# A two-layer gated DeltaNet and Conformer encoder on one core: the small-tile products of two delta steps stand side by side, and the filling comes in three groups a step

## Chip, core and metric

One core of one Trainium2 chip. The metric is the device time of one execution in microseconds (us). A core has a matrix engine (TensorE, PE in the rows; PEld is its weight load), a vector engine (VectorE, DVE), an engine for functions of one operand (ScalarE, ACT), a general one (GpSimd, POOL) and one that issues transfers (SyncE, SP). Each takes its instructions in order from its own queue; semaphores tie them together. Operands lie in SBUF, products arrive in PSUM.

## What is computed

Two layers over 2048 tokens of width 1024. Each has an input projection, a bidirectional gated DeltaNet (4 heads of 128), a Conformer convolution branch, gates, two output projections and a residual sum. The change lies in the DeltaNet's scan over chunks, which the reference writes so:

```python
lmat = jnp.where(strict, jnp.einsum('bhncd,bhnsd->bhncs', k_beta, k) * decay, 0.0)
sol = lax.linalg.triangular_solve(eye + lmat, rhs, left_side=True, lower=True, unit_diagonal=True)
value, k_cum = sol[..., :dv], sol[..., dv:]
attn = jnp.einsum('bhncd,bhnsd->bhncs', q, k) * decay
...
def step(state, inp):
    val_n, kc_n, a_n, qd_n, kd_n, dl_n = inp
    v_new = val_n - jnp.einsum('bhcd,bhde->bhce', kc_n, state)
    o_n = jnp.einsum('bhcd,bhde->bhce', qd_n, state) + jnp.einsum('bhcs,bhse->bhce', a_n, v_new)
    state = state * dl_n[..., None, None] + jnp.einsum('bhcd,bhce->bhde', kd_n, v_new)
    return state, o_n
```

It runs once forward and once backward, and the two outputs are added, normalised and gated.

## The kernel before

The layer first makes all projections (`head`, `conformer`, `act_tile`, `gates(0)`), then runs `delta`, then `merge`. Wide products are split into three f32r matmuls of 128x512 (lines 185 to 187: high times high, high times low, low times high) for each 128 rows of the contraction.

`delta` takes 128 tokens per chunk and works in 16 steps; step s treats chunk s forward and chunk 15-s backward. Three kinds of generators are advanced by hand in the loop, and that written order is bound on TensorE, ScalarE, VectorE and GpSimd (`bind`); the transfers of SP are placed by the scheduler.

- `lane(step, d, ...)`, one per direction, is the scan itself: pk and pq (keys and queries times the state, L989 and L992), the x update on VectorE (L994) and o1 on ScalarE (L998); from step 8 on a sum on GpSimd (L1001) with the output that the other direction left for this chunk; pw (the inverse times x, L1005) and its copy to vn (L1007); pn and po (L1014, L1023), the state update (L1017) and the output sum (L1025 or L1030).
- `prep(i)` makes the inverse of the 128x128 triangular matrices of step i from the inverses of its 32x32 blocks, ahead of time. Its pieces are: loads; masks on GpSimd (L907); exponentials on ScalarE (L913); then transposes (L917), copies (L923, and pp on L925) and products with the decays (L927, L929); then four small-tile phases on TensorE: z1 (32x32, L936), do (32x32, L946 and L949), z2 (64x64, L960 and L961), d2 (64x64, L969 and L970), each followed by copies out of PSUM (L939; L951 to L955; L963; L971 and L972). Each `go(i)` advances prep(i) by one piece.
- `finish(pair)` from step 8 on normalises two finished outputs: squares on ScalarE (L1044); one step later the rsqrt chain on VectorE (L1054, L1055, L201 to L207, L1058), the scaling on ScalarE (L1062), and transposes on TensorE (L1067) with the gate's product on VectorE (L1068).

Between them `pull(n)` takes n filling units out of other work: the second half of the gates, then the first part of the merge. A unit is three 128x512 matmuls. Eight of them make one output tile (evicted by L829 on ScalarE, with a store issued there, L153), and every sixteen a new weight is split into halves, by ScalarE (L159) and VectorE (L160).

All products but the filling use one pool of five PSUM tiles (pz) in turn; the filling has three of its own (pd). The operands of prep lie in rings: two steps of keys (rgk), three of queries (rgq), two of row decays (rgb), three of inverses (rwt).

Of the kernel before, what the change touches and what calls it, by code (L numbers as in the profile page):

```python
# [27 lines left out]
GAP = 0  # L28
SPLITS = (245, 247, 249, 250, 251, 252, 253, 254)
LEAD = (8, 10, 6, 6, 6, 4)  # L30
STEP = (4, 4, 4, 4)
TAIL = (2, 2, 1, 4, 8)
Z = '121'
PART = 5
# [44 lines left out]
class Trunk:  # L79
# [754 lines left out]
    def delta(self):  # L834
        nc = self.nc
# [6 lines left out]
        def ring(cols, n):  # L842
            out = []
            for _ in range(n):
                slot = next(x for x in left if x[2] - x[1] >= cols)
                out.append(slot[0][:, slot[1]:slot[1] + cols])
                slot[1] += cols
            return Ring(out)

        rkq, rkv = ring(1024, 4), ring(1024, 4)  # L850
        rgq, rgk = ring(NB, 6), ring(NB, 4)
        rwt = ring(1024, 3)
        rgb, ro1, rvn, ro, rza, rst, dp = (ring(NB, n) for n in (4, 2, 2, 5, 2, 2, 2))
# [5 lines left out]
        hv = lambda t: t.rearrange("p (h c) -> p h c", h=4)  # L859

        def fetch(step):
            out = []
            for d in range(2):
                c = step if d == 0 else NCH - 1 - step
                kq = rkq().rearrange("p (h a c) -> p h a c", h=4, a=2)
                kv = rkv().rearrange("p (a h c) -> p a h c", h=4, a=2)
                self.load(kq, self.kq_d[c])
                self.load(kv, self.kv_d[c])
                out.append((c, kq, kv))
            return out  # L870

        def decay_keys(ins, d):
            c, _, kv = ins
            k2 = col(self.kf, d, c)
            nc.gpsimd.tensor_tensor(out=kv[:, 0], in0=kv[:, 0], in1=k2[:, :, None].to_broadcast([P, 4, P]),
                                    op=ALU.mult)
# [7 lines left out]
        def prep(step):  # L884
            ins, ks, gbs = [], [], []
# [2 lines left out]
            pt = dpt[:, 256:512].rearrange("p (d h c) -> p d h c", d=2, h=4)  # L888
            chunk = (step, NCH - 1 - step)
            for d, c in enumerate(chunk):  # L890
                g, k, gb = hv(rgq()), hv(rgk()), hv(rgb())
                with nc.allow_non_contiguous_dma(reason="rows to all partitions and inverse blocks"):
                    r0 = d * 64 + c * 4
                    self.load(gb, self.gc_d[r0:r0 + 4][None].to_broadcast([P, 4, P]))
                    self.load(k, self.g_d[c][:, :, 0, :])
                    self.load(g, self.g_d[c][:, :, 1, :])
                    r4 = 64 * d + 4 * c
                    self.load((dt if d == 0 else pt)[:, d],
                              self.inv_d[:, r4:r4 + 4, :].rearrange("h b (i j) -> (b i) h j", j=32))
                ins.append(g)  # L900
                ks.append(k)
                gbs.append(gb)
            yield
            for d, c in enumerate(chunk):
                gb = gbs[d]
# [3 lines left out]
            for d, c in enumerate(chunk):  # L909
                gb = gbs[d]  # L910
# [10 lines left out]
            for b in range(4):  # L921
                r = blk(b)
                v_.tensor_copy(wt[r, :, 32 * b:32 * b + 32], dtm[r])  # L923
                d, q = (0, 32 * b) if b < 2 else (1, 32 * (b - 2))
# [150 lines left out]
        def pull(n):  # L1075
            for _ in range(n):
                if next(fill, GAP) == GAP:
                    return

        start = self.mark()  # L1080
        nil = iter(())
        preps = [prep(i) for i in range(NCH)] + [nil, nil, nil]
        go = lambda i: next(preps[i], None)
        go(0)
        ins = fetch(0)
        pull(LEAD[0])
        go(0)
        go(0)
        go(0)
        go(1)  # L1090
        pull(LEAD[1])
        go(0)
# [3 lines left out]
        pull(LEAD[2])  # L1096
        go(1)
        go(0)
        pull(LEAD[3])
        go(1)  # L1100
        go(0)
        go(2)
        pull(LEAD[4])
        ready = go(0)
        pull(LEAD[5])
        last = finish([])
        for step in range(NCH):
            nxt = fetch(step + 1) if step + 1 < NCH else None
            gs, wt = ready
            lanes = [lane(step, d, gs[d], wt, *ins[d]) for d in range(2)]  # L1110
            for x in lanes:
                next(x)
            go(step + 1)
            go(step + 2)
            for x in lanes:
                next(x)
            if nxt:
                for d in range(2):
                    decay_keys(nxt[d], d)
            next(last)  # L1120
            pull(STEP[0])
            for x in lanes:
                next(x)
            go(step + 2)
            next(last)
            go(step + 1)
            pull(STEP[1])
            for x in lanes:
                next(x, None)
            go(step + 1)  # L1130
            go(step + 2)
            go(step + 3)
            new = finish(list(done))
            done.clear()
            if step == NCH - 1:
                break
            if step < LATE_SQUARES:
                next(new)
            pull(STEP[2])
            if step >= LATE_SQUARES:  # L1140
                next(new)
            next(last)
            ready = go(step + 1)
            last = new
            pull(STEP[3])
            ins = nxt
        for n, part in zip(TAIL, (new, last, new, new, new)):
            pull(n)
# [351 lines left out]
```

## Time and profile before

| | |
|---|---|
| median of three runs | 3140.98 us (3136.1 to 3143.68) |
| profiled execution, its time | 3143.1 us |
| its span, first to last instruction | 3141.3 us |
| TensorE clock granted over the span | 0.995 |
| delta stage, layer 1: first pw of step 0 | at 910.8 us |
| delta stage, layer 2: first pw of step 0, of step 15 | at 2447.5 and 2787.5 us |

A row of the timeline reads: start, duration, engine, line, operation, output <- input, shape, count; in brackets the engine's idle time before it and what ended that. A PE duration is longer than the distance to the next start, since matmuls are pipelined: distances of starts are what counts there. A row of a single line gives minimum/median/maximum duration in ns. In the chain each row is start, duration and line of a piece of the work that ended last.

### The profile page before, as it was taken

The numbers are of one execution on the slowest core, as the hardware profiler recorded it, in microseconds if no ns is written. First come the engines' busy times: TensorE is split into PE (matmuls) and PEld (weight loads), VectorE is DVE, ScalarE is ACT, GpSimd is POOL, SyncE is SP. The second block draws the span as 40 slices with busy tenths as digits, with TensorE's granted clock in tenths as the row PEclk, the third lists the DMA queues.
The fourth block names the chain that finished last, engine by engine and source line by source line (L and its number), as shares of the span: only waits on it lengthen the run. The fifth ranks groups of instructions, "written<-read, shape, count | busy, mean of one in ns | idle before, by whom it ended". The sixth has DMA issues, their size and how long they took to land. (4 is left out here: it accounts for less than half of the span.)

```text
span 3141.3 us, 51438 instructions
## 1 busy us (share of the span) xinstructions
PE 3077.3 (98%) x19190; PEld 2707.1 (86%) x19190; DVE 2400.3 (76%) x4441; ACT 1377.3 (44%) x3074; POOL 297.9 (9%) x297
## 2 busy tenths in 40 slices
PE   6999999999999999999999999999999999999998
PEld 5888888888889998888888888888888899988887
DVE  7789898997556698746666989999955567877665
ACT  5625152522454466434345252525234545644342
POOL 3000000000032222000000000000001212200000
PEclk9999999999999999999999999999999999999999
DMA  4233222234587787655413141414347878965643
GB/s 147 90 95 95 88 91 91 89 111 137 194 297 253 250 266 237 198 188 141 152 35 106 67 124 58 121 61 119 124 158 258 269 234 266 290 201 189 216 159 124
DMA packets 429417, 501.71 MB, mean 160 GB/s; under 512 B 96432, under 2 KB 262960, under 8 KB 429168
## 3 DMA queue, kind: packets, MB, share of 16 engines
q1 hardware_dynamic: 351232, 380.19, 38.8%
q10 hardware_dynamic: 69872, 88.48, 8.0%
q0 software_dynamic: 8064, 29.76, 2.5%
q8 instruction: 151, 2.47, 0.3%
q14 instruction: 98, 0.80, 0.1%
HBM read 342.74 MB, written 155.58 MB: 159 GB/s over the span
## 5 line engine op out<-in xcount | busy, mean ns | idle before, releaser
L185 PE MATMUL pd<-h,whi 128*128 128x512 f32 x2816 | 1092.3, 388 | 0.0
L187 PE MATMUL pd<-h,wlo 128*128 128x512 f32 x2816 | 1070.5, 380 | 1.5 <-DVE wlo L160 1.5
L186 PE MATMUL pd<-h,whi 128*128 128x512 f32 x2816 | 1070.9, 380 | 0.0
L749 DVE SCALAR_TENSOR_TENSOR cacc<-gp,vec,cacc 128x1009 f32<-128x1009 f32 (+1 forms) x480 | 615.7, 1283 | 29.6 <-ACT cacc L747 26.6
L185 PEld LDWEIGHTS pd<-h,whi 128*128 128x128 f32 x2816 | 534.1, 190 | 79.5 <-issue 1.4
L187 PEld LDWEIGHTS pd<-h,wlo 128*128 128x128 f32 x2816 | 533.7, 190 | 78.6 <-DVE wlo L160 2.3
L186 PEld LDWEIGHTS pd<-h,whi 128*128 128x128 f32 x2816 | 534.0, 190 | 72.6 <-issue 1.9
L159 ACT ACTIVATE whi<-wraw 128x512 fp32r<-128x512 f32 x394 | 239.3, 623 | 478.6 <-PE pd L186 352.6
L160 DVE TENSOR_TENSOR wlo<-wraw,whi 128x512 fp32r<-128x512 f32 x394 | 267.8, 693 | 116.9 <-ACT whi L159 115.2
L574 DVE SCALAR_TENSOR_TENSOR acc<-cin,vec,acc 128x1022 f32<-128x1022 f32 (+1 forms) x192 | 246.5, 1299 | 13.9 <-ACT acc L572 12.6
L187 PE MATMUL pd<-yhi,wlo 128*128 128x512 f32 x488 | 185.6, 380 | 4.6 <-DVE wlo L160 4.5
L185 PE MATMUL pd<-yhi,whi 128*128 128x512 f32 x488 | 185.5, 380 | 0.7 <-ACT whi L159 0.7
L186 PE MATMUL pd<-ylo,whi 128*128 128x512 f32 x488 | 185.0, 379 | 0.0
L829 ACT ACTIVATE go<-pd,vec 128x512 f32<-128x512 f32 x128 | 87.3, 682 | 130.9 <-PE pd L187 116.6
L550 ACT ACTIVATE cin<-pd 128x512 f32<-128x512 f32 x96 | 56.8, 593 | 152.3 <-PE pd L187 152.1
L761 ACT ACTIVATE ao<-pd 128x512 f32<-128x512 f32 x64 | 38.3, 599 | 193.9 <-PE pd L187 193.8
L187 PEld LDWEIGHTS pd<-yhi,wlo 128*128 128x128 f32 x488 | 92.2, 189 | 19.5 <-DVE wlo L160 6.6
L185 PE MATMUL pd<-uop,whi 128*128 128x512 f32 x256 | 100.2, 391 | 5.1 <-ACT whi L159 5.1
L185 PEld LDWEIGHTS pd<-yhi,whi 128*128 128x128 f32 x488 | 92.2, 189 | 14.3 <-ACT whi L159 1.5
L186 PEld LDWEIGHTS pd<-ylo,whi 128*128 128x128 f32 x488 | 92.2, 189 | 12.9
L187 PE MATMUL pd<-uop,wlo 128*128 128x512 f32 x256 | 98.0, 383 | 0.1
L186 PE MATMUL pd<-uop,whi 128*128 128x512 f32 x256 | 97.8, 382 | 0.0
(312 smaller groups left out, 4814.9 us busy)
## 6 DMA issues: line engine op xcount, KB each, us to landing
wraw<-w_in SPq DMA_DIRECT2D x240, 256.0 KB, 3.5
gt<-go ACTq DMA_DIRECT2D x128, 256.0 KB, 4.2
dl<-gr SPq DMA_DIRECT2D x128, 256.0 KB, 5.3
dl<-kq SPq DMA_DIRECT2D x64, 512.0 KB, 6.3
dl<-kv SPq DMA_DIRECT2D x64, 512.0 KB, 5.7
wraw<-w_out SPq DMA_DIRECT2D x90, 256.0 KB, 3.0
kq<-acc SPq DMA_DIRECT2D x16, 1024.0 KB, 5.4
gr<-go ACTq DMA_DIRECT2D x64, 256.0 KB, 2.2
```

What stands on the lines that cost most here:

```text
L159: self.nc.scalar.activation(hi, src, AF.Copy)
L160: self.nc.vector.tensor_tensor(out=lo, in0=src, in1=hi.bitcast(F32), op=ALU.subtract)
L185: mm(ps, whi[:, k, :], xhi, start=k == 0, stop=False)
L186: mm(ps, whi[:, k, :], xlo, start=False, stop=False)
L187: mm(ps, wlo[:, k, :], xhi, start=False, stop=k == kk - 1)
L550: nc.scalar.activation(cut(t[:, o + b * NB:o + (b + 1) * NB]), sort(ps), AF.Copy)
L574: self.nc.vector.scalar_tensor_tensor(out=out, in0=t[:, k:k + n], scalar=wc(k), in1=out, op0=ALU.mult, op1=ALU.add)
L749: self.nc.vector.scalar_tensor_tensor(out=acc, in0=t[:, k:k + n], scalar=wc(k), in1=acc, op0=ALU.mult, op1=ALU.add)
L761: nc.scalar.activation(cut(o), sort(ps), func)
L829: nc.scalar.activation(cut(o), sort(ps), AF.Identity if half else AF.Sigmoid, bias=self.vec[:, V_GB + j:V_GB + j + 1])
```

## The change

Prep's loads become two pieces (the row decays first, then k, queries and inverse blocks), so that prep has nine pieces for eight. The loop advances them in another order, and a step's sixteen filling units come as 6, 5 and 5 in place of 4, 4, 4 and 4. The start of the stage is rewritten to match.

```diff
-STEP = (4, 4, 4, 4)
+STEP = (6, 5, 5)
...
             for d, c in enumerate(chunk):
-                g, k, gb = hv(rgq()), hv(rgk()), hv(rgb())
+                gb = hv(rgb())
...
                     self.load(gb, self.gc_d[r0:r0 + 4][None].to_broadcast([P, 4, P]))
+                gbs.append(gb)
+            yield
+            for d, c in enumerate(chunk):
+                g, k = hv(rgq()), hv(rgk())
...
                     self.load(k, self.g_d[c][:, :, 0, :])
                     self.load(g, self.g_d[c][:, :, 1, :])
...
             for x in lanes:
                 next(x)
-            go(step + 1)
             go(step + 2)
             for x in lanes:
                 next(x)
             if nxt:
                 for d in range(2):
                     decay_keys(nxt[d], d)
+            go(step + 2)
             next(last)
             pull(STEP[0])
             for x in lanes:
                 next(x)
-            go(step + 2)
+            go(step + 3)
             next(last)
-            go(step + 1)
             pull(STEP[1])
             for x in lanes:
                 next(x, None)
             go(step + 1)
             go(step + 2)
             go(step + 3)
...
             next(last)
+            go(step + 2)
             ready = go(step + 1)
+            go(step + 3)
             last = new
-            pull(STEP[3])
```

In step s the loop now makes of prep(s+2) the exponentials, then the transposes, copies and products, then z1 and do; of prep(s+1) z2 and d2; of prep(s+3) both loads and the masks.

TensorE in one step of layer 1, before, from the output products (L1023) to pw (L1005) of the next step; rows of L185 to L187 are filling:

```order
L1023 MATMUL pz<-dm_6983,dl_6981 128x128 x4
L960 MATMUL pz<-dh_6988,dl_6981 64x64
L961 MATMUL pz<-dh_6988,dl_6981 64x64
...
L185 MATMUL pd<-h_395,whi 128x512
...
L969 MATMUL pz<-dl_6981,dh_6989 64x64
L970 MATMUL pz<-dl_6981,dh_6989 64x64
...
L185 MATMUL pd<-h_395,whi 128x512
...
L992 MATMUL pz<-dh_6987,dl_6980 128x128 x4
L936 MATMUL pz<-dh_6987,dl_6981 32x32 x16
```

The same stretch now (every line behind the loads carries a number four higher: z2 is L964 and L965, z1 L940, do L950 and L953, d2 L973 and L974, pk L993):

```order
L1027 MATMUL pz<-dm_6983,dl_6981 128x128 x4
L964 MATMUL pz<-dh_6988,dl_6981 64x64
L965 MATMUL pz<-dh_6988,dl_6981 64x64
...
L940 MATMUL pz<-dh_6987,dl_6981 32x32 x16
L185 MATMUL pd<-h_395,whi 128x512
...
L953 MATMUL pz<-dh_6989,dh_6987 32x32 x2
L973 MATMUL pz<-dl_6981,dh_6989 64x64
L974 MATMUL pz<-dl_6981,dh_6989 64x64
...
L993 MATMUL pz<-dh_6986,dl_6980 128x128 x4
```

z1 has moved from behind pq to behind z2, do from behind pw to just ahead of d2, and no filling is left between d2 and the next step's pk.

VectorE in a late step of layer 1 (step 9), before, from the x update to the copies of d2:

```order
L994 SCALAR_TENSOR_TENSOR dl_6980<-pz,neg,dl_6980 128x128 x8
L1054 TENSOR_TENSOR oss<-oss,cq_1007 128x8
...
L1058 TENSOR_TENSOR orr<-orr,cq 128x8
L951 COPY dh_6988<-pz 32x4x32
...
L1017 SCALAR_TENSOR_TENSOR dh_6986<-dh_6986,dl,pz 128x128 x4
...
L917 STREAM_TRANSPOSE dh_6988<-dh_6988 128x128 x2
L923 COPY dl_6981<-dh_6988 32x8x32 x4
L927 TENSOR_TENSOR dl_6981<-dl_6981,dm_6982 128x512 x2
L929 TENSOR_TENSOR dl_6981<-dl_6981,dm_6982 128x512 x2
L160 TENSOR_TENSOR wlo<-wraw,whi 128x512 x2
L1068 SCALAR_TENSOR_TENSOR dh_6985<-pz,vec,dh_6985 128x512
```

And now:

```order
L998 SCALAR_TENSOR_TENSOR dl_6980<-pz,neg,dl_6980 128x128 x8
L921 STREAM_TRANSPOSE dh_6988<-dh_6988 128x128 x2
L927 COPY dl_6981<-dh_6988 32x8x32 x4
L931 TENSOR_TENSOR dl_6981<-dl_6981,dm_6982 128x512 x2
L933 TENSOR_TENSOR dl_6981<-dl_6981,dm_6982 128x512 x2
L1058 TENSOR_TENSOR oss<-oss,cq_1007 128x8
...
L1062 TENSOR_TENSOR orr<-orr,cq 128x8
L160 TENSOR_TENSOR wlo<-wraw,whi 128x512 x2
L1021 SCALAR_TENSOR_TENSOR dh_6986<-dh_6986,dl,pz 128x128 x4
...
L1072 SCALAR_TENSOR_TENSOR dh_6985<-pz,vec,dh_6985 128x512
...
L955 COPY dh_6988<-pz 32x4x32
```

The transposes, copies and products stand ahead of the rsqrt chain, and the weight split (L160) ahead of the state update.

ScalarE in the same step, before, from vn (L1007) to the next eviction:

```order
L1007 ACTIVATE dm_6983<-pz 128x512 x2
L913 ACTIVATE dm_6982<-dm_6982,ngc 128x128 x8
L1062 ACTIVATE dm_6984<-dm_6984,orr 128x128 x8
L829 ACTIVATE go<-pd,vec 128x512
...
L963 ACTIVATE dh_6989<-pz 128x256
L925 ACTIVATE dh_6988<-dh_6988 32x4x32 x4
...
L159 ACTIVATE whi<-wraw 128x512 x2
```

And now, from the exponentials:

```order
L917 ACTIVATE dm_6982<-dm_6982,ngc 128x128 x8
L929 ACTIVATE dh_6988<-dh_6988 32x4x32 x4
L1011 ACTIVATE dm_6983<-pz 128x512 x2
L1066 ACTIVATE dm_6984<-dm_6984,orr 128x128 x8
L829 ACTIVATE go<-pd,vec 128x512
...
L159 ACTIVATE whi<-wraw 128x512 x2
L967 ACTIVATE dh_6989<-pz 128x256
L943 ACTIVATE dh_6989<-pz 128x128
L1048 ACTIVATE junk,oss<-dh_6985 128x128 x4
```

The exponentials and pp come ahead of vn, and the weight's first half (L159) ahead of the squares (L1044, now L1048), right behind the scaling and an eviction.

More of the change, by code (lines that the diff above doesn't have):

```diff
@@ L890, in prep @@
             for d, c in enumerate(chunk):
-                g, k, gb = hv(rgq()), hv(rgk()), hv(rgb())
-                with nc.allow_non_contiguous_dma(reason="rows to all partitions and inverse blocks"):
+                gb = hv(rgb())
+                with nc.allow_non_contiguous_dma(reason="rows to all partitions"):
                     r0 = d * 64 + c * 4
                     self.load(gb, self.gc_d[r0:r0 + 4][None].to_broadcast([P, 4, P]))
+                gbs.append(gb)
+            yield
+            for d, c in enumerate(chunk):
+                g, k = hv(rgq()), hv(rgk())
+                with nc.allow_non_contiguous_dma(reason="inverse blocks"):
                     self.load(k, self.g_d[c][:, :, 0, :])
@@ L901, in prep @@
                 ks.append(k)
-                gbs.append(gb)
             yield
@@ L1084, in delta @@
         go(0)
+        go(0)
         ins = fetch(0)
@@ L1089, in delta @@
         go(0)
+        go(1)
         go(1)
@@ L1098, in delta @@
         go(0)
+        go(1)
         pull(LEAD[3])
+        go(0)
         go(1)
-        go(0)
+        go(2)
         go(2)
@@ L1104, in delta @@
         ready = go(0)
+        go(1)
+        go(2)
         pull(LEAD[5])
```

## The prediction

> **What bounds the kernel now.** I read the page's engine shares first, then TensorE's timeline through one step of the delta stage, then VectorE's, ScalarE's and GpSimd's timelines through a late step, then the waits and the chain.
>
> ```profile
> PE 3077.3 (98%) x19190; PEld 2707.1 (86%) x19190; DVE 2400.3 (76%) x4441; ACT 1377.3 (44%) x3074; POOL 297.9 (9%) x297
> ```
>
> TensorE is busy nearly throughout, so only two things can move the time: how tightly its instructions follow each other, and the few places where it waits. The change touches TensorE's order in the two delta stages alone (16 steps each).
>
> ```profile
> 2455.32 1.06 PE L1023 MATMUL pz<-dm,dl 128*128 128x128 f32 x8
> 2456.31 0.27 PE L960 MATMUL pz<-dh,dl 64*64 64x64 f32 x1
> ...
> 2456.77 0.22 PE L961 MATMUL pz<-dh,dl 64*64 64x64 f32 x1
> 2456.92 0.48 PE L185 MATMUL pd<-h,whi 128*128 128x512 f32 x1
> 2457.24 0.38 PE L186 MATMUL pd<-h,whi 128*128 128x512 f32 x1
> 2457.46 0.38 PE L187 MATMUL pd<-h,wlo 128*128 128x512 f32 x1
> ```
>
> This is one small-tile phase, z2, between full-width work. Eight L1023 at 0.11 us each end at 2456.21; the first 64x64 matmul starts 0.10 us later. After the last one 0.15 us pass, and the first filling matmul holds TensorE 0.32 us where its successor takes 0.22: 0.10 more. The phase thus costs 0.81 us (2456.21 to 2457.02), of which its sixteen matmuls stream for about 0.47. **About 0.34 us is getting in and out.**
>
> The late steps look different:
>
> ```profile
> 2647.77 1.78 PE pz L1005 x16
> ...
> 2717.66 1.78 PE pz L1005 x16
> 2740.77 1.80 PE pz L1005 x16
> ...
> 2765.17 1.78 PE pz L1005 x16
> ```
>
> These pieces of the chain are the pw products of steps 9, 12, 13 and 14. From 12 to 13 a step takes 23.11 us with TensorE never waiting; from 9 to 12 the three take 69.89, 0.5 more than three such; from 13 to 14 24.40, 1.3 more. **So 1.8 us per layer are lost to waits in late steps already.** One of them has its name in the waits:
>
> ```profile
> PE pz L989 <- DVE dh L1068: 0.8, 1, 0.8
> ```
>
> The pool of five pz tiles is used in turn: a state product (L989) had to wait until VectorE had read the transposed output (L1068) out of the tile five before it. VectorE, ScalarE and GpSimd around that place:
>
> ```profile
> 2644.14 1.27 POOL L1001 TENSOR_TENSOR dm<-dm,dm 128x512 f32<-128x512 f32 x1 [14.75 <-ACT dm L998]
> 2645.92 1.27 POOL L1001 TENSOR_TENSOR dh<-dh,dm 128x512 f32<-128x512 f32 x1 [0.51 <-ACT dm L998]
> 2647.15 2.04 POOL L875 TENSOR_TENSOR dl<-dl,kf 128x512 f32<-128x512 f32 x2
> 2649.15 2.51 POOL L907 TENSOR_TENSOR dm<-dm,con 128x512 f32<-128x512 f32 x2
> ```
> ```profile
> 2645.95 1.27 DVE L205 TENSOR_TENSOR rst<-orr,rsv 128x8 f32<-128x8 f32 x1
> ...
> 2652.51 0.17 DVE L1058 TENSOR_TENSOR orr<-orr,cq 128x8 f32<-128x8 f32 x1
> ...
> 2654.55 1.12 DVE L1017 SCALAR_TENSOR_TENSOR dh<-dh,dl,pz 128x128 f32<-128x128 f32 x4
> ...
> 2657.82 0.50 DVE L917 STREAM_TRANSPOSE dh<-dh 128x128 f32<-128x128 f32 x2
> ...
> 2660.77 1.29 DVE L929 TENSOR_TENSOR dl<-dl,dm 128x512 f32<-128x512 f32 x2
> 2663.43 1.29 DVE L160 TENSOR_TENSOR wlo<-wraw,whi 128x512 fp32r<-128x512 f32 x2 [1.37 <-ACT whi L159]
> 2664.64 1.41 DVE L1068 SCALAR_TENSOR_TENSOR dh<-pz,vec,dh 128x512 f32<-128x512 f32 x2
> ...
> 2666.83 2.16 DVE L994 SCALAR_TENSOR_TENSOR dl<-pz,neg,dl 128x128 f32<-128x128 f32 x8
> ```
> ```profile
> 2652.72 2.45 ACT L1062 ACTIVATE dm<-dm,orr 128x128 f32<-128x128 f32 x8 [0.19 <-DVE orr L1058]
> 2655.07 0.67 ACT L829 ACTIVATE go<-pd,vec 128x512 f32<-128x512 f32 x1
> 2655.77 0.33 ACTq L153 DMA_DIRECT2D gt<-go  x1
> ```
> ```profile
> L159 ACT ACTIVATE whi<-wraw 128x512 fp32r<-128x512 f32 x394 | 239.3, 623 | 478.6 <-PE pd L186 352.6
> ```
>
> VectorE has one pause of 1.37 us in this step. And an op on eight columns (L205) took 1.27 us, as long as the GpSimd sum beside it, where its like later takes 0.17: **while GpSimd works on SBUF, VectorE gets in one op per GpSimd op.** The large ops suffer too (minimum/median/maximum ns in layer 1's delta stage):
>
> ```profile
> L929 DVE TENSOR_TENSOR dl<-dl,dm x30: 677/686/1521, 903.3 to 1221.0; 128x512 f32<-128x512 f32 x30
> L907 POOL TENSOR_TENSOR dm<-dm,con x28: 1264/1272/1727, 899.8 to 1183.5; 128x512 f32<-128x512 f32 x28
> ```
>
> [...]
>
> **Part by part.** (1) *Fewer ways in and out.* Nothing is added or removed on TensorE; 16 filling units per step stay 16 (6+5+5 for 4x4). z2 of one step now stands directly before z1 of the next, and do before d2: two joins in each of steps 0 to 13 and two in the lead, 30 per layer, 60 in all. A join saves one way into small tiles (0.10 us) and one slow first full-width matmul (0.10); the 0.15 us after the last small matmul I keep, since 64x64 and 32x32 are still different tiles. That is 0.20 us, **-12 us** in all. No row shows 64x64 beside 32x32. A join removes a border and adds none, so its bounds are 0 and the phase's whole 0.34 us: 0 to -20 us. I take the middle because it keeps what the row shows after any small phase.
>
> [...]
>
> (2) *Products of the decays ahead of pw.* Two transposes, four copies and four products (L917 to L929) move from behind the state update to behind the x update (L994). In early steps they fill a hole:
>
> ```profile
> 2472.39 0.28 DVE L951 COPY dh<-pz 32x128 f32<-32x128 f32 x1 [5.37 <-ACT dm L1007]
> ```
>
> Their 4.2 us (2657.82 to 2661.98) fit into those 5.4. The state update's cover before the next step's first product is z2, z1, five units (15 x 0.22), do and d2: some 5.5 us, where VectorE has only it and the output sum to do (3.3 us for both directions, 2654.55 to 2657.82); without that cover the step would take what is left of the 3.3. The loads, now in two portions, wait on SP for their buffers as before; SP's next entries behind them are the state's own loads, a step early. The last buffer freed is that of k, by z2; until its product stand z1, five units, do, d2 and four state products (3.6): some 9 us, against the landing time of
>
> ```profile
> dl<-gr SPq DMA_DIRECT2D x128, 256.0 KB, 5.3
> ```
>
> I cost (2) and the loads at nothing in steps 0 to 8.
>
> (3) *Late steps.* From step 9 VectorE's order is x update, transposes, copies, products, rsqrt chain (14 small ops), weight split (L160), state update, L1068, copies of do and d2. The weight split moves ahead of the state update because filling unit 48 now falls into the second group; on ScalarE its first half (L159) stands behind the scaling L1062, which waits for the rsqrt chain. So a loop closes: za (L1068) frees the pz tile that the first L992 of the next step needs, now with no filling between. Its length, from the end of the first L1068: second L1068 and d2 copies 1.5 (2664.64 to 2666.83, less the first 0.66), do copies 1.85 (2652.7 to 2654.55), x updates 2.1: **5.5**. The transposes, copies and products: 4.2 alone. But GpSimd's second sum starts when o1 of the second direction is scaled; its product waits for the do copies (2.5), so that is at about 4.6 (0.9 and 1.1 later), and the sum (1.27) holds VectorE until 5.9, and decays and masks (2.04 and 2.51) until 10.4, in which VectorE gets in five of its ten ops. The other five, a copy and the four products, take 2.7, and GpSimd, held up in turn, adds some 0.5 by the 1.7 of its longest op: ready at 13.6, so **8.1**. Rsqrt 14 x 0.20: **2.7**. Scaling, eviction and its DMA issue 3.4 (2652.72 to 2656.10), one L159 0.6: **4.0**. Split 1.21, state update with sums 3.27 (2654.55 to 2657.82), first L1068 0.66: **5.1**. Sum **25.5 us**, while TensorE needs 23.1 - 0.4 = 22.7.
>
> TensorE's new idle time per layer: step 9, entered with VectorE in time, 1.3; steps 10 and 11, 2.8 each; 12, without a weight split, 0.7 (the fourth state product waits for the do copies); 13, with eight splits in a row, 1.5; 14, 0.7. That is 9.8, less the 1.8 lost there before: **+16 us** for both layers.
>
> **Sum:** -12 + 16 = +4 us. The profiled execution took 3143.1 us (span 3141.3), 2.1 above the median of the three runs, 3140.98; on the median I get **3145 us**.
>
> **Rivals.** *A, only TensorE counts.* If the moved ops slip past GpSimd's (their 8.1 become 4.2), the loop is 21.6 us and late steps are bound by TensorE: -12, and the old 3.6 us of waits go too, 3125 us. For it: 677 ns is the common duration of the product. Against it: in late steps GpSimd's seven microseconds start exactly behind o1. *B, slower through the loop.* If VectorE and GpSimd alternate strictly, each GpSimd op stretched to the 1.7 us of the row above, five of them add 2.3 us to every loop of steps 9 to 13: +20 us, less what step 9 and 12 can hide, some +14: 3159 us. From a loop of 25.8 us on, the whole is more than 0.2% slower. *C, joins save nothing.* Going from 64x64 to 32x32 costs what leaving and entering cost: 3157 us. *D, the joins save all 0.34 us*: 3137 us.
>
> **How the numbers follow.** Forecast 0.46 (3139 to 3150 by itself), A 0.22, B 0.17, C 0.10, D 0.05. The range takes in A's time and reaches to B and C: 3124 to 3157 leaves out some 0.2. About 0.2% (6.3 us) is what a measurement of this kernel can tell from no change. Faster by more: A and a little of the forecast, 0.27. Slower by more: B, C and the forecast's upper part, 0.37. Within: 0.36.
>
> **What would show it.** Steps 1 to 8 should be 0.4 us shorter from pw to pw than before, TensorE without a wait; no gain would make C right, 0.7 D. Steps 10 and 11 should take 25.5 us, with L992 waiting for L1068; 22.7 makes A right, over 27 B. In them L927 and L923's like should show maxima near 1.3 us beside GpSimd's ops, and wlo should wait for whi. Waits of TensorE in steps 1 to 8, for pp, vn or a late load, would show that (2) isn't free, and make the prediction wrong from a side that I hold unlikely.

## The result and the profile after

The changed kernel takes 3195.6 us (median of four runs, 3185.92 to 3197.22), the kernel before 3142.33 us beside it; the ratio is 1.0166 (95% interval 1.0141 to 1.0192). It is slower by 53 us, where 4 us were forecast with a range up to 3157 us.

The page of the changed kernel, its first lines:

```profile
span 3194.7 us, 51372 instructions
PE 3088.4 (97%) x19190; PEld 2718.2 (85%) x19190; DVE 2435.9 (76%) x4441; ACT 1375.5 (43%) x3074; POOL 314.7 (10%) x297
```

The span grew by 53.4 us (3141.3 before). TensorE's idle time, span less busy time, went from 64.0 to 106.3 us: 42.3 of them. The other 11.1 are busy time, with the same number of instructions: some of them run slower. TensorE's waits in the changed kernel (us in total, times, longest) say where the idle time is; those that only the delta stages have, or that grew there:

```profile
PE pz L940 <- ACT dh L967: 24.9, 6, 4.4
PE pd L187 <- DVE wlo L160: 12.8, 8, 3.9
PE pd L185 <- ACT whi L159: 11.0, 5, 4.5
PE pz L940 <- DVE dl L931: 2.8, 2, 1.4
PE pz L940 <- DMA dl<-kq: 2.8, 2, 1.4
PE pz L950 <- ACT dh L943: 2.4, 2, 1.3
```

L940 is z1, L967 the copy of z2 out of its tile: z1 waits six times, some 4.2 us each, for the z2 ahead of it. Before, z1 waited for nothing, and the two rows of weight splits (L187 for L160, L185 for L159) had 6.0 and 5.8 us.

To place the loss I set the filling matmuls of the two traces side by side, the n-th of one against the n-th of the other. The lead of each delta stage costs 4.6 us more; steps 0 to 8 gain 3.1 us per layer; from there to the last step 22.4 (layer 1) and 20.8 us (layer 2) are lost; behind the last step 4.4 and 3.0. These make 53.5; outside the delta stages the two traces drift by 3 us either way and come out even.

One small-tile phase of an early step in TensorE's timeline (start, duration):

```profile
947.45 0.22 PE L965 MATMUL pz<-dh,dl 64*64 64x64 f32 x1
947.60 0.45 PE L940 MATMUL pz<-dh,dl 32*32 32x32 f32 x32
947.98 0.48 PE L185 MATMUL pd<-h,whi 128*128 128x512 f32 x1
948.30 0.38 PE L186 MATMUL pd<-h,whi 128*128 128x512 f32 x1
```

From the last 64x64 matmul to the first 32x32 one 0.15 us pass, what passed before full-width work; one way in and one slow first filling matmul are gone. A step from pw to pw takes 21.84 us in place of 22.23: 0.39 for two joins.

The same join at the end of step 10, and what follows:

```profile
1151.32 0.22 PE L965 MATMUL pz<-dh,dl 64*64 64x64 f32 x1
1155.91 0.75 PE L940 MATMUL pz<-dh,dl 32*32 32x32 f32 x32 [4.37 <-ACT dh L967]
1156.59 0.80 PE L185 MATMUL pd<-h,whi 128*128 128x512 f32 x1
1157.17 0.63 PE L186 MATMUL pd<-h,whi 128*128 128x512 f32 x1
...
1162.24 0.38 PE L186 MATMUL pd<-h,whi 128*128 128x512 f32 x1
1162.46 0.38 PE L187 MATMUL pd<-h,wlo 128*128 128x512 f32 x1
1162.68 0.60 PE L1071 MATMUL pz<-con,dh 128*128 128x128 f32 x4
```

z1 starts 0.06 us after the z2 eviction ends and reads nothing that the eviction writes: what it waits for is z2's own tile of the five. Then the filling goes at one matmul per 0.43 us for 5 us, and only from 1162.24 at the 0.22 of everywhere else: **behind the wait TensorE runs at half speed**, 12 matmuls at 0.21 too much, 2.5 us. The granted clock says the same (window, sum, PE busy, its matmuls and so on to the clock, the third number from the end):

```profile
1156.00:1163.00 7.00, 7.00 (x50) 5.70 (x51) 3.66 (x11) 3.37 (x17) 0.00 (x0) 0.56 0.49 150
```

Summed over both delta stages such spells cost the filling some 19 us (2 before). Less these 2 and the 6 us that the joins gain in early steps, that is the 11 us by which busy time grew, a rough account: what the spells cost z1 and the state products, and what joins gain in late steps, is not in it. In the changed kernel each of the nine waits of 3.8 to 4.5 us in the delta stages and their tails was followed by such a spell (granted clock 0.50 to 0.60 over the 4 us behind the wait). Of the shorter waits some were (2.73 us in the kernel before, 2.08 in e6, 2.43 in e2) and some were not (1.28 in the changed kernel, with a clock of 1.00 over the 4 us behind it; 1.59 in e1; 2.41 in e2). The spell is not bound to filling either: in e5, behind waits of a state product (L993), the granted clock was 0.50 from 1128.5 to 1131.5 us (wait of 2.89) and 1.00 from 1156.6 to 1160.0 (wait of 2.44).

Why z2's eviction is so late, from VectorE and then ScalarE in the same step:

```profile
1133.12 1.41 DVE L1072 SCALAR_TENSOR_TENSOR dh<-pz,vec,dh 128x512 f32<-128x512 f32 x2 [3.15 <-PE pz L1071]
...
1139.36 0.49 DVE L921 STREAM_TRANSPOSE dh<-dh 128x128 f32<-128x128 f32 x2
1139.89 1.18 DVE L927 COPY dl<-dh 32x256 f32<-32x256 f32 x4
1141.11 3.10 DVE L931 TENSOR_TENSOR dl<-dl,dm 128x512 f32<-128x512 f32 x2
1144.13 3.21 DVE L933 TENSOR_TENSOR dl<-dl,dm 128x512 f32<-128x512 f32 x2
1147.26 1.23 DVE L1058 TENSOR_TENSOR oss<-oss,cq 128x8 f32<-128x8 f32 x1
...
1155.10 1.29 DVE L160 TENSOR_TENSOR wlo<-wraw,whi 128x512 fp32r<-128x512 f32 x2 [4.12 <-ACT whi L159]
1156.31 1.12 DVE L1021 SCALAR_TENSOR_TENSOR dh<-dh,dl,pz 128x128 f32<-128x128 f32 x4
...
1163.32 1.41 DVE L1072 SCALAR_TENSOR_TENSOR dh<-pz,vec,dh 128x512 f32<-128x512 f32 x2 [3.66 <-PE pz L1071]
```
```profile
1151.02 1.28 ACT L1066 ACTIVATE dh<-dh,orr 128x128 f32<-128x128 f32 x4 [6.27 <-DVE orr L1062]
...
1154.44 1.15 ACT L159 ACTIVATE whi<-wraw 128x512 fp32r<-128x512 f32 x2 [0.40 <-ACT go L829]
1155.49 0.36 ACT L967 ACTIVATE dh<-pz 128x256 f32<-128x256 f32 x1
```

Read as one loop from the first L1072 (over at about 1133.8) to the next: copies and x update until 1139.36, 5.6 us; transposes, copies and products beside GpSimd until 1147.34, 8.0; rsqrt chain until 1151.0, 3.7; scaling, eviction, two weight splits and z2's eviction until 1155.85, 4.9; then z1, five filling units, the transposes and the first L1072 until about 1164.0, 8.1. Together 30.2, and from pw of step 10 to pw of step 11 it is 30.20. VectorE stands still for 4.1 and 3.7 us in it: nobody is full, the loop is long.

### The profile page after: what moved, and what is told of

Same layout as the page of the kernel before. It is cut to its first block, busy times and chain, and to the rows that moved or that the text cites. A ratio compares the mean times of both kernels' runs of the same rounds, so it can differ in the third digit from the quotient of the medians.

```text
span 3194.7 us, 51372 instructions
## 1 busy us (share of the span) xinstructions
PE 3088.4 (97%) x19190; PEld 2718.2 (85%) x19190; DVE 2435.9 (76%) x4441; ACT 1375.5 (43%) x3074; POOL 314.7 (10%) x297
## 5 line engine op out<-in xcount | busy, mean ns | idle before, releaser
L185 PE MATMUL pd<-h,whi 128*128 128x512 f32 x2816 | 1094.7, 389 | 0.0
L187 PE MATMUL pd<-h,wlo 128*128 128x512 f32 x2816 | 1076.2, 382 | 1.8 <-DVE wlo L160 1.8
L187 PEld LDWEIGHTS pd<-h,wlo 128*128 128x128 f32 x2816 | 536.5, 191 | 80.9 <-DVE wlo L160 3.0
L185 PEld LDWEIGHTS pd<-h,whi 128*128 128x128 f32 x2816 | 538.2, 191 | 76.6 <-issue 1.2
L159 ACT ACTIVATE whi<-wraw 128x512 fp32r<-128x512 f32 x394 | 239.2, 623 | 494.4 <-PE pd L186 353.4
L160 DVE TENSOR_TENSOR wlo<-wraw,whi 128x512 fp32r<-128x512 f32 x394 | 267.3, 692 | 151.4 <-ACT whi L159 150.9
L574 DVE SCALAR_TENSOR_TENSOR acc<-cin,vec,acc 128x1022 f32<-128x1022 f32 (+1 forms) x192 | 246.3, 1298 | 13.7 <-ACT acc L572 12.5
L187 PE MATMUL pd<-yhi,wlo 128*128 128x512 f32 x488 | 185.7, 381 | 4.6 <-DVE wlo L160 4.5
L185 PE MATMUL pd<-yhi,whi 128*128 128x512 f32 x488 | 185.6, 380 | 2.5 <-ACT whi L159 2.5
L185 PE MATMUL pd<-uop,whi 128*128 128x512 f32 x256 | 101.7, 397 | 8.5 <-ACT whi L159 8.5
L187 PEld LDWEIGHTS pd<-yhi,wlo 128*128 128x128 f32 x488 | 92.2, 189 | 19.9 <-DVE wlo L160 7.0
L187 PE MATMUL pd<-uop,wlo 128*128 128x512 f32 x256 | 100.7, 394 | 6.6 <-DVE wlo L160 6.4
L1002 ACT ACTIVATE dm<-pz,eg 128x128 f32<-128x128 f32 x240 | 68.6, 368 | 89.1 <-PE pz L996 89.1
L185 PEld LDWEIGHTS pd<-yhi,whi 128*128 128x128 f32 x488 | 92.2, 189 | 16.7 <-ACT whi L159 4.1
```

The source lines that it names most:

```text
L159: self.nc.scalar.activation(hi, src, AF.Copy)
L160: self.nc.vector.tensor_tensor(out=lo, in0=src, in1=hi.bitcast(F32), op=ALU.subtract)
L185: mm(ps, whi[:, k, :], xhi, start=k == 0, stop=False)
L187: mm(ps, wlo[:, k, :], xhi, start=False, stop=k == kk - 1)
L574: self.nc.vector.scalar_tensor_tensor(out=out, in0=t[:, k:k + n], scalar=wc(k), in1=out, op0=ALU.mult, op1=ALU.add)
L1002: nc.scalar.activation(hv(o1)[:, hd, :], pq[:, hd, :], AF.Copy, scale=eg[:, hd:hd + 1])
```

## Experiments

All steps are compared from pw to pw, in layer 1; "9" is from step 9 to step 10. Times are one run each where no interval stands; the kernel before took 3141 to 3143 us beside them.

| kernel | early | 9 | 10 | 11 | 12 | 13 | time, us |
|---|---|---|---|---|---|---|---|
| before | 22.23 | 23.10 | 23.30 | 23.48 | 23.10 | 24.41 | 3142 |
| changed | 21.84 | 29.14 | 30.20 | 28.73 | 23.36 | 29.43 | 3195.6 |
| e1, scaling behind z1 | 21.84 | 24.00 | 24.37 | 24.18 | 22.96 | 29.61 | 3163.9 |
| e2, rsqrt first | 21.84 | 26.90 | 30.18 | 28.74 | 24.63 | 29.24 | 3195.3 |
| e3, one join undone | 22.04 | 25.20 | 27.57 | 25.25 | 22.95 | 28.64 | 3164.5 |
| e4, lead's groups | 21.84 | 29.26 | 30.27 | 28.75 | 23.30 | 29.41 | 3192.1 |
| e5, splits in third group | 21.84 | 28.83 | 25.23 | 27.50 | 22.71 | 27.43 | 3164.3 |
| e6, masks on VectorE | 21.84 | 26.65 | 27.59 | 27.63 | 22.72 | 30.14 | 3182.0 |
| e7, e1 with e5 and lead | 21.84 | 27.78 | 27.52 | 27.52 | 22.72 | 25.06 | 3159.6 |
| e8, late z1 ahead | 21.84 | 25.93 | 27.54 | 27.09 | 22.92 | 30.14 | 3164.5 |
| e9, joins early only | 21.84 | 23.11 | 23.48 | 23.56 | 23.10 | 24.41 | 3135.8 |
| e10, products only | 22.23 | 25.08 | 26.95 | 25.02 | 26.85 | 29.51 | 3176.3 |

**e1: the scaling behind z1.**

```diff
             go(step + 3)
-            next(last)
             pull(STEP[1])
...
             go(step + 2)
             go(step + 3)
+            next(last)
             new = finish(list(done))
```

> The changed kernel with one edit: the scaling of the finished pair (L1066, eight ops of ScalarE) is issued behind z2 and z1 of a step, not ahead of the second group of filling. Theory T (tile): in steps 9 to 11 z1 stands ahead of five filling units and takes the pz tile of the z2 just before it, which ScalarE frees behind scaling, an eviction and two weight splits; with the scaling behind it, z1 waits only for the state update behind the weight split, some 2 us in place of 4.2, no half-speed spell of the filling follows, and steps 9 to 11 take 24 to 25 us in place of 29.3. Total about 3165 us. Rival R (lock): the loop of the prediction through VectorE, GpSimd and scaling sets the step by itself, wherever the scaling stands; steps 9 to 11 stay at 28 us or more, total about 3190 us.

Measured 3163.92 us, steps 9 to 11 at 24.0 to 24.4. z1 now waits for the state update alone (TensorE's rows):

```profile
1146.88 0.45 PE L940 MATMUL pz<-dh,dl 32*32 32x32 f32 x32 [1.59 <-DVE dh L1021]
1150.61 0.60 PE L1071 MATMUL pz<-con,dh 128*128 128x128 f32 x4
```

1.6 us, and no half-speed spell: z1 to transposes takes 3.7 us in place of 6.8. (In layer 2 step 10 had a spell, behind 1.67 us, and took 26.14.) As the tile theory said; the rival, that the loop is the same wherever the scaling stands, falls: scaling now runs beside the five filling units. Step 13 is untouched, so its loss is another.

**e2: the rsqrt chain ahead of the products.**

```diff
-            go(step + 2)
             next(last)
+            go(step + 2)
             pull(STEP[0])
```

> The changed kernel with one edit: the rsqrt chain of the finished pair (fourteen small VectorE ops) is issued ahead of the transposes, copies and products of the decays in a step, not behind them. Theory T: scaling then starts some 8 us earlier, ScalarE is through with the weight splits before z2, z1 waits only for the state update behind products and split, 1 to 2 us in place of 4.2; steps 9 to 11 take 23.5 to 24.5 us, step 13 loses its wait for the weight split; total 3155 to 3165 us. Rival R: VectorE's work and the lock are the same in sum, the state update ends as late as now, steps 9 to 11 stay within 1.5 us of 29.3, total about 3190 us.

Measured 3195.32 us: nothing gained. The tile theory was wrong here. z1's wait did fall, to 2.4 us, but a new one stands ahead of it, and VectorE's rows show why the loop is no shorter:

```profile
1166.85 0.15 DVE L1058 TENSOR_TENSOR oss<-oss,cq 128x8 f32<-128x8 f32 x1
...
1174.15 0.50 DVE L921 STREAM_TRANSPOSE dh<-dh 128x128 f32<-128x128 f32 x2
...
1177.10 1.29 DVE L933 TENSOR_TENSOR dl<-dl,dm 128x512 f32<-128x512 f32 x2
```
```profile
1176.51 1.13 PE L1018 MATMUL pz<-dm,dl 128*128 128x128 f32 x8 [1.68 <-ACT dm L1011]
1183.37 0.62 PE L940 MATMUL pz<-dh,dl 32*32 32x32 f32 x32 [2.43 <-DVE dh L1021]
```

Now the rsqrt chain takes 7.3 us beside GpSimd (1166.85 to 1174.15) and transposes to products 4.2 behind it: 11.5 together, against 8.0 and 3.7 in the changed kernel. The delay falls on whichever ops stand there: five of the fourteen small ones took 0.96 to 1.26 us each in place of 0.17. And the pp copies (L929) on ScalarE now wait for the transposes with vn's eviction (L1011) queued behind them, which the state products need. So this swap inside the loop gained nothing. That only what leaves the loop shortens it became the theory (loop) for the rest.

**e3: one of a step's two joins undone.**

```diff
             go(step + 1)
+            pull(3)
             go(step + 2)
             go(step + 3)
             new = finish(list(done))
...
-            pull(STEP[2])
+            pull(STEP[2] - 3)
```

> The changed kernel with one edit: three of the five filling units of the third group stand between z2 and z1 of each step, two behind z1, so that one of the two joins of a step is undone. Theory T: early steps take 0.20 us more (22.04 in place of 21.84, half of the 0.39 that two joins saved); in steps 9 to 11 the three units (1.95 us) hide that much of z1's wait, it falls from 4.2 to about 2.3 and the half-speed spell with it: 25 to 27 us; total about 3180 us. Rival R: late steps unchanged within 0.5 us, total about 3200 us.

Measured 3164.5 us. Early steps take 22.04: **one join is worth 0.20 us**, half of 0.39. In late steps z1's waits are 1.67, 2.81 and 1.72 us; only behind the 2.81 does the half-speed spell show, and that step is the 27.57. Three units taken from between z1 and the transposes give 2.6 to 3.9 us per step, more than their own 1.95, because the spells go too. The total came out 15.5 us under the expected 3180; of it some 3 us are drift ahead of the first delta stage.

**e4: the lead's groups.**

```diff
-LEAD = (8, 10, 6, 6, 6, 4)
+LEAD = (8, 10, 8, 8, 4, 2)
```

> The changed kernel with one edit: the groups of filling of the lead are 8, 10, 8, 8, 4, 2 in place of 8, 10, 6, 6, 6, 4 (40 in both). Theory T: the lead's 4.5 us per layer are three waits of TensorE (1.1, 1.4, 1.4 us) and the half-speed spell behind them; with two and four units more ahead of them the waits fall to under 1 us in sum and the spell goes: 4 to 4.5 us less per layer, total about 3187 us, steps unchanged. Rival: the products of step 1 wait for loads that wait in turn for buffers that the filling frees, so the waits move along with the units: no change.

Measured 3192.05 us, 5 more than expected and within the range of the changed kernel's own runs, so only the trace tells. The lead's loss went from 4.6 to 0.7 us in layer 1 and to 2.1 in layer 2, steps unchanged. Its waits are two products of step 1 that z1 needs two groups earlier than before, and behind them the spell:

```profile
900.97 0.24 PE L940 MATMUL pz<-dh,dl 32*32 32x32 f32 x2 [1.43 <-DMA dl<-kq]
902.64 0.58 PE L940 MATMUL pz<-dh,dl 32*32 32x32 f32 x30 [1.42 <-DVE dl L931]
903.15 0.79 PE L185 MATMUL pd<-h,whi 128*128 128x512 f32 x1
903.73 0.63 PE L186 MATMUL pd<-h,whi 128*128 128x512 f32 x1
```

(rows of the changed kernel; the first names a DMA, but starts as the first L931 ends.) The waits do not move along with the units, as the rival had it.

**e5: every weight split in the third group.**

```diff
-LEAD = (8, 10, 6, 6, 6, 4)
+LEAD = (8, 10, 6, 6, 6, 1)
```

> The changed kernel with one edit: the lead holds 37 filling units in place of 40 (8, 10, 6, 6, 6, 1), so that every weight split falls behind z2 and z1, in the third group, as in the kernel before, and not in the second. Theory T (tile and loop): ahead of the z2 eviction ScalarE no longer has two splits, ahead of the state update VectorE none; z1's wait in steps 9 to 11 falls from 4.2 to 2 to 3 us and the steps to 26 to 28 us; step 13, where TensorE waited 3.9 us for the split of the next weights, takes 23 to 25 us in place of 29.4; total about 3172 us. Rival: the split's wait moves with it (the third group's filling waits for a split that stands behind the state update): steps 9 to 11 and 13 within 1 us of now, total 3190 us.

Measured 3164.34 us, 8 less than expected. z1's wait is gone (0.2 us), and in its place the first state product waits for L1072, as the prediction had it but one product earlier (L993, where it named L992, now L996): 2.89, 2.44 and 2.95 us in steps 9 to 11. Half speed followed the first and the third (granted clock 0.50 and 0.53, 1.00 behind the second): from L993 to the next pw 10.5, 7.6 and 9.1 us pass, which is most of why these steps take 28.8, 25.2 and 27.5 us. Behind the last step 1.4 and 2.9 us fewer than before are spent, where the changed kernel lost 4.4 and 3.0: that loss, too, was the split's place. Step 13 gains 2 us only; z1 there waits 2.3 us for z2's tile.

**e6: the masks on VectorE.**

```diff
-                nc.gpsimd.tensor_tensor(out=gb, in0=gb, in1=msk[:, None, :].to_broadcast([P, 4, P]), op=ALU.add)
+                v_.tensor_tensor(out=gb, in0=gb, in1=msk[:, None, :].to_broadcast([P, 4, P]), op=ALU.add)
```

> The changed kernel with one edit: the two masks of a step (L911) are added by VectorE, not by GpSimd. Theory T: of GpSimd's work beside transposes, copies and products of late steps (sum, decays, masks: 8.0 us from the first transpose to the last product) the masks' share goes, so that these take 5.5 to 6.5 us; the 1.3 us of the masks come back on VectorE ahead of the x update, in the same loop; steps 9 to 11 take 27.5 to 29 us in place of 29.3; early steps unchanged if VectorE has the 1.3 us to spare; total 3180 to 3192 us. Rival (GpSimd does not set the loop): the ten ops take as long as now, steps 9 to 11 take 30 us or more, total 3200 us.

Measured 3181.95 us; steps 9 to 11 average 27.3 in place of 29.4. VectorE in step 10:

```profile
1132.21 1.29 DVE L911 TENSOR_TENSOR dm<-dm,con 128x512 f32<-128x512 f32 x2
...
1135.62 0.50 DVE L921 STREAM_TRANSPOSE dh<-dh 128x128 f32<-128x128 f32 x2
1136.15 3.41 DVE L927 COPY dl<-dh 32x256 f32<-32x256 f32 x4
1139.59 1.30 DVE L931 TENSOR_TENSOR dl<-dl,dm 128x512 f32<-128x512 f32 x2
1140.80 1.29 DVE L933 TENSOR_TENSOR dl<-dl,dm 128x512 f32<-128x512 f32 x2
```

Transposes to products take 6.5 us in place of 8.0. The products take their undisturbed 1.29 per pair in place of 3.10 and 3.21; the copies now stand beside GpSimd and take 3.41 in place of 1.18. GpSimd's share of the loop is real; the masks' 1.3 us on VectorE eat most of it, and shorter waits with shorter spells give the rest.

**e7: e1 with the splits in the third group and another lead.** The edit of e1, and

```diff
-LEAD = (8, 10, 6, 6, 6, 4)
+LEAD = (8, 10, 8, 8, 3, 0)
```

> The changed kernel with three edits: scaling behind z2 and z1, all weight splits in the third group (37 units in the lead), and the lead's groups 8, 10, 8, 8, 3, 0. Theory T: each takes away its own part: steps 9 to 11 at 23 to 23.7 us, step 13 at 23 to 24 us, the lead 3 to 4 us per layer shorter than in the changed kernel; total 3138 to 3146 us. Rival: the parts cover each other, one wait takes the place of another: 3155 us or more.

Measured 3159.59 us, 14 more than the theory's upper end; the rival was right. Steps 9 to 11 are back at 27.5:

```profile
1146.59 1.26 ACT L1066 ACTIVATE dh<-dh,orr 128x128 f32<-128x128 f32 x4
1147.76 1.27 ACT L1066 ACTIVATE dm<-dm,orr 128x128 f32<-128x128 f32 x4
1152.27 1.13 ACT L159 ACTIVATE whi<-wraw 128x512 fp32r<-128x512 f32 x2
```
```profile
1152.91 1.29 DVE L160 TENSOR_TENSOR wlo<-wraw,whi 128x512 fp32r<-128x512 f32 x2 [5.04 <-ACT whi L159]
1154.12 1.40 DVE L1072 SCALAR_TENSOR_TENSOR dh<-pz,vec,dh 128x512 f32<-128x512 f32 x2
```
```profile
1154.92 1.46 PE L993 MATMUL pz<-dh,dl 128*128 128x128 f32 x7 [3.11 <-DVE dh L1072]
```

In the third group the split waits on ScalarE behind scaling and squares, VectorE waits for it 5 us with L1072 queued behind, and L993 waits for L1072. Two edits that each gave 31 us alone give 36 with a better lead besides: each moves the place where the loop catches TensorE. Behind the wait shown the clock is 0.57 until 1158.5: it slows the state products here.

**e8: from step 8 on z1 ahead of the state products, lead as in e7.**

```diff
             pull(STEP[1])
+            if step >= 8:
+                go(step + 2)
             for x in lanes:
                 next(x, None)
             go(step + 1)
-            go(step + 2)
+            if step < 8:
+                go(step + 2)
```

> The changed kernel with two edits: from step 8 on z1 stands ahead of the state products, behind the second group of filling, apart from z2 (early steps keep both joins); the lead's groups are 8, 10, 8, 8, 3, 0, so that the weight splits fall in the third group. Theory T: z1 then takes a tile that neither scaling nor state update frees, the filling behind z2 is not held, no half-speed spells; steps 9 to 13 at 22.8 to 23.8 us, total 3134 to 3144 us. Rival: z1 now waits for the products themselves, which end as late as the state products start, and the wait stays at 2 us or more: steps 9 to 11 at 25 us or more, total 3150 us or more.

Measured 3164.45 us. z1 no longer waits, nor does it wait for the products, as the rival had it; L993 waits for L1072 again, 2.5 to 2.7 us (clock 1.00 behind the one of step 9, 0.56 behind that of step 10, which takes 1.6 us more), and in step 13 z2 waits 4.3 us for the state update. Neither expectation had the place; the rival had the size.

**e10: the moved products alone.** In the kernel before, exp, transposes, copies and products go ahead of pw and the masks to the end of a step; no join, four groups of four.

```diff
             if nxt:
                 for d in range(2):
                     decay_keys(nxt[d], d)
+            go(step + 2)
             next(last)
...
-            go(step + 2)
             next(last)
             go(step + 1)
             pull(STEP[1])
...
             go(step + 1)
-            go(step + 2)
             go(step + 3)
...
             ready = go(step + 1)
+            go(step + 3)
```

> The kernel before with one part of the change: exp, transposes, copies and products of a step stand ahead of pw (behind the x update), masks at the end of a step; no joins, four groups of four, lead as before. Theory T: without z1 and its five units behind the state update the loop of late steps is x update, products 8.0, rsqrt chain 3.6, weight split and state update, L1068: 23.3 to 25.5 us for steps 9 to 11, early steps 22.23 as before, total 3142 to 3155 us; so the joins, not the moved products alone, make most of the 50 us. Rival: the products beside GpSimd make them alone: steps 9 to 11 at 28 us or more, total 3180 us or more.

Measured 3176.3 us: **33 of the 53 us come with the moved products alone**, 29.4 of them in the steps from 9 on (16.0 us in layer 1, 13.4 in layer 2); lead and early steps together are within 1.1 us per layer of before, and the rest of the 33 is these and drift outside. I had expected at most 14, the rival at least 39: neither holds. Here the loop catches TensorE at a third place:

```profile
1146.55 1.13 PE L1023 MATMUL pz<-dm,dl 128*128 128x128 f32 x8 [1.97 <-DVE dh L952]
```
```profile
1145.62 0.17 DVE L1058 TENSOR_TENSOR orr<-orr,cq 128x8 f32<-128x8 f32 x1
1146.12 0.29 DVE L952 COPY dh<-pz 32x128 f32<-32x128 f32 x1
```

The last output product starts as the second of do's copies (L951 to L955) ends, and these stand behind products and rsqrt chain on VectorE; by which tile it depends on that copy, the rows do not show. The remaining 20 us come with the rest of the change, the joins and the groups of 6, 5 and 5 that move the weight splits: some 8 in the two leads, the rest in late steps and the tail, less 6 gained early. Such shares do not add up to a split of blame: undoing one join alone (e3) takes 31 of the 53 us away too.

**e9: the change in the early steps alone.** Lead and steps from 9 on in the order of before, steps 0 to 7 joined, z1 and do of step 1 in step 0's old places. The core of the loop, the parts that differ from both:

```diff
+            late = step >= APART
+            join = step + 1 < APART
+            n0, n1, n2, n3 = (4, 4, 4, 4) if late else (6, 5, 5, 0)
...
+            if late or step == 0:
+                go(step + 1)
+            if step != APART:
+                go(step + 2)
...
+            if not late:
+                go(step + 2)
             next(last)
...
+            go(step + (2 if late else 3))
             next(last)
+            if late or step == 0:
+                go(step + 1)
...
             go(step + 1)
+            if late or join:
+                go(step + 2)
             go(step + 3)
+            if late:
+                go(step + 3)
```

with APART = 9.

> The changed kernel in steps 0 to 8, the kernel before in the lead and from step 9 on: both joins, the groups 6, 5, 5 and the products ahead of pw in steps 0 to 7 (step 8 leaves out z1 and do of step 10), four groups of four and the products behind the state update from step 9 on, the lead as before. Theory T: eight steps per layer gain 0.39 us each and nothing is paid in the lead, in late steps or in the tail: 6 us less than before, total 3133 to 3138 us beside a before of 3141, ratio 0.997 to 0.999. Rival: going from one order to the other and back costs what the joins gain (a late load or product in steps 0, 8 or 9): 3140 us or more.

Measured 3135.76 us (median of 11 runs) beside 3142.23, ratio 0.9978 (0.9969 to 0.9987): **faster than both kernels**, by the joins' gain and no more. The trace has 21.84 in steps 1 to 7, 23.1 to 24.4 in steps 9 to 13; in layer 1's delta stage TensorE waits for little:

```profile
PE pd L185 <- ACT whi L159: 2.7, 2, 1.7
PE pz L950 <- ACT dh L943: 1.5, 1, 1.5
PE pz L993 <- DVE dh L1072: 1.0, 2, 0.8
```

## Why the prediction was wrong

**Fewer ways in and out: right.** Forecast 0.20 us per join, with the 0.15 behind the last small matmul kept; measured 0.39 for two, 0.20 for one (e3), and the 0.15 stands in the row (947.45 to 947.60). But the sum counted 60 joins as gains, and in the lead and from step 9 on a join is where TensorE waits.

**Moved products and loads at nothing in steps 0 to 8: right for the steps, not for the lead.** No wait in steps 0 to 8 of either layer. The lead was not costed at all, though the change moves z1 and do of step 1 forward there: 4.6 us per layer, 2.8 of them waits (three, less the one of before) and 1.2 to 1.7 half speed (e4).

**The late steps: the loop was right, its end was not.** "So a loop closes: za (L1068) frees the pz tile that the first L992 of the next step needs" is the step that failed. Of its five terms the first two had the right size, 5.5 and 8.1 against 5.6 and 8.0. The second was partly luck: GpSimd's second sum began 7.1 us into the loop and not 4.6, its last mask ended at 14.7 and not 10.4, and it was the four products that GpSimd slowed (3.10 and 3.21 per pair), the copies not at all. Rsqrt was written as 2.7 (14 x 0.20 is 2.8, and the sum 25.5 has 2.8) and measured 3.7, because GpSimd still held its first op for 1.2; the ScalarE term was 4.0 and measured 4.9, with two weight splits in it and not one. The last, 5.1 for split, state update and first L1068, took the transposes as done by then. They were not: on TensorE they stand behind z1 and five filling units, and z1 waits for z2's tile, which ScalarE frees last of all. This term is 8.1, half speed included. The loop is 30.2 and not 25.5, and it catches TensorE at z1, not at the state products. Where the split or z1 is moved away (e5, e7, e8), it does catch them, as forecast but for one product.

**The idle time per layer.** Forecast 9.8 for steps 9 to 14. The waits of these steps in layer 1 sum to 17.0 (three of z1 with 12.5, z1 in step 12 with 0.6, step 13 with 3.9), and the half-speed spells behind them add 6.8. The trace of before had such a spell in view, ten matmuls at 0.43 us behind a wait of 2.73 in layer 2's tail, and it stands in no term. Step 13 was put at 1.5: there a filling matmul in the second group needs a split that stands behind products and rsqrt on VectorE. It waits 3.9 us, and the step takes 29.4 us in place of 24.4.

**The tail** was costed at nothing and took 4.4 and 3.0, with the splits' place (e5).

**The rivals.** B, a slower loop, had the direction, and by its sign (steps 10 and 11 over 27 us) it came true; but its mechanism did not, since the ten ops beside GpSimd took 8.0 us and not the 10.4 that strict alternation adds up to, and it went only to 3159; no rival had a wait put ahead of filling, nor a wait that slows what comes behind it. That the moved products alone do harm, 33 us (e10), the prediction had in its late steps, at half the size; that joins cost 9 in the lead and more late, it had nowhere.

## What to carry to other kernels

When work is joined to save a border, look at what the second part waits for and at what then stands behind it: filling that used to cover a wait is queued behind it instead, and becomes part of the loop. Follow such a loop to the place where it meets the bound engine, term by term and through the engine's own order (the transposes here), and count what is queued between. And where a loop has several places to catch the bound engine, moving one wait away brings up the next: keep the change where it has slack (here steps 0 to 7, e9) and leave the rest as it was.

## What the runs showed of the hardware

A wait of TensorE can cost more than its length: behind z1's waits of 3.8 to 4.4 us in the changed kernel 4 to 12 filling matmuls started 0.43 us apart in place of 0.22, 0.9 to 2.5 us on top. The granted clock was 0.50 there (from 1157 to 1162 us, for one). Shorter waits had it or had it not at the same length: 2.43 us with, 2.41 without, both in e2 (clock 0.53 and 1.00 behind them).

The delay that GpSimd laid on VectorE stayed with the place and not with the op: ten large ops took 8.0 us beside it, and when fourteen small ones stood there they took 7.3 in place of 2.6 (1141.92 to 1144.5 in e1), while the large ones took 4.2.
